# A two-layer hybrid attention trunk on one core: wider modulation products, a scaling moved to ScalarE, staggered value loads, and another scheduler for all instructions

## The chip, the core and the metric

The kernel runs on one core of one Trainium2 chip. The metric is the device time of an execution in microseconds (us). The core has TensorE (PE, matrix products; PEld are its weight loads), VectorE (DVE), ScalarE (ACT), GpSimd (POOL) and SyncE (SP), which here issues the DMAs. Each engine works through its own list of instructions strictly in order.

## What is computed

Two layers of a decoder trunk, sequence 512, width 1024, float32. Each layer, cut to what matters:

```python
shift, scale, gate = split(silu(c) @ w_ada + b_ada, 3)
h = rms_norm(x, ln_pre) * (1 + scale) + shift
u = split_columns(h @ w_in)          # 3740 columns: groups a, b, c, d
o_a = dilated_attention(a_q, a_k, a_v)
o_b = nsa_attention(b_q, b_kc, b_vc, b_ks, b_vs, b_kw, b_vw, b_g, ...)
o_c = rms_norm(gla_attention(c_q, c_k, c_v, log_sigmoid(c_a @ w_a2 + b_a) / 16), gla_norm)
o_d = banded_attention(d_q, d_k, d_v, window 128, sinks)
mixed = concat(o_a * silu(a_z), o_b * silu(b_z), o_c * silu(c_z), o_d * silu(d_z))
x = x + gate * rms_norm(mixed @ w_out, ln_post)
```

Group B compresses its keys and values by a small two-layer network (weights `w1`, `w2`) before it attends to them.

## The kernel before, in words

Every large product is made of three matmuls in a reduced-precision float form: the operand is split into a rounded part (`hi`) and a remainder (`lo`), and hi*hi, hi*lo and lo*hi are summed. So each piece of a weight (`wraw`, 128 x 1024 for most) is loaded, cast to `whi` on ScalarE (L475) and subtracted to `wlo` on VectorE (L478). The activations stand as `HH` and `HL`, transposed. `raw` holds four such loaded pieces, `w` three pairs of split ones.

**Start-up of layer 0** (`startup`, L659). x comes in four tiles of 128 rows. Each is squared and summed on ScalarE (L421), its reciprocal root is made on VectorE and GpSimd (L425, L426), and the tile is scaled on VectorE (L676). TensorE transposes it (L703), and the modulated result becomes `HH` and `HL` (L709 to L711). Shift and scale come from `mod` (L285): VectorE multiplies a weight tile `wmod` of 128 x 512 by the row silu(c) and sums it (L290), two halves for each of 16 columns. The weights of group C's first projections are used at once (`mms`, L719, L723).

**Projections** (`proj`, L641). 24 matmuls for each piece of 128 output columns (`mm_T`, L525), in the order of the list `CHUNKS`. While they run, the groups' attention is worked out.

**Group C** (`attn_c`, L811), gated linear attention without a sequential scan: six levels (64, 32, 16, 8, 4, 2 positions). At each level VectorE and ScalarE make decayed keys and queries `kq` (L922 to L926), TensorE makes scores `att` (L932), they are masked (L941), and TensorE multiplies them by values `vs` (L953). These values stand in another order than the projection leaves them: the projection's result goes to DRAM (`vd`, L571) and comes back as `vs`, two DMAs for each level (L824), all twelve issued at the start of the group. Ahead of the levels stands the log decay `la` (L836, L837) and its running sum `bp` (L841).

**Softmax units** (`unit`, L744): scores `sc` (L638, L639), mask and maximum on VectorE (L755), exponential on ScalarE (L757), scaling on VectorE (L766, L768), transposes `pT` on TensorE (L771), copies (L776, L778).

**Compression of group B** (`attn_b`, L1038): four `w1` loads fill the four raw buffers, TensorE makes `hid` (L1052), transposes it to `hT` (L1061), VectorE and ScalarE work out the gelu in some ten small steps on `hbuf`, TensorE makes `kcp` (L1080) and, from its split copy `kc`, the compressed scores `scmp` (L1097).

**Output** (`out1`, `out2`): the output projection `yo`, the second norm, the residual, the next layer's norm, transposes (L454) and its first projection (`mmTM`, L536). Norm of group C: `ms` (L972) from the split square `lo`.

**Background.** `extras` (L359) makes the next layer's modulation (32 products of `wmod`, L290) and this layer's gate (16 steps of `wada`, L348, L350) in small units with two buffers (`ad`).

**What sets the order.** The program is written in Python in a merged order: `merge` interleaves the groups with the projections by costs (the numbers after `yield` and the table `LP`). Then the tile scheduler reorders it: among instructions whose inputs are ready in its own model of the core, it takes the one with the best priority (program order, shifted by `tc.cur_priority`), engine by engine. The result is a fixed list for each engine and for SyncE's DMAs. `TLS = False` selects the scheduler's simple model of time; L1355 passes it on.

Of the kernel before, what the change touches and what calls it, by code (L numbers as in the profile page):

```python
# [19 lines left out]
PRE = 2  # L20
TLS = False
B = dict(raw=4, w=3, mx=3, v4=5, dv=2, ad=2, qk=16, g=8, p=3, sz=4, pt=3, sm=4)
QT = QH = QL = QG = 0
QX = 60
FIRST = 'xCwPxwxwxwTQc'
XH = 2
SG, MG = 1, 2
# [154 lines left out]
def pack(inp):  # L182
# [8 lines left out]
    for l in range(DEPTH):  # L191
# [10 lines left out]
        w_gate[l] = wa[:, 2048:].reshape(8, 128, 2, 512).transpose(2, 0, 1, 3)  # L202
        w_mod[l] = wa[:, :2048].reshape(2, 512, 2, 8, 128).transpose(3, 2, 0, 4, 1)
        for i, n in enumerate(('nsa_w1_k', 'nsa_w1_v')):
# [26 lines left out]
def build(tc, A, out_d):  # L231
    nc = tc.nc
    PE, ACT, DVE, POOL, SP = nc.tensor, nc.scalar, nc.vector, nc.gpsimd, nc.sync
    with ExitStack() as ctx:
# [44 lines left out]
        def load_mod(l, n, p, tag):  # L279
# [3 lines left out]
            return wt  # L283

        def mod(l, n, wt, ss, gs):  # L285

            o, c = _P['bada'][0], n // 2
            h = n % 2
            init, dst = (tmp[:, c:c + 1], ss[:, c:c + 1]) if h else (pars[l][:, o + c:o + c + 1], tmp[:, c:c + 1])
            DVE.tensor_tensor_reduce(wt, wt, csr[:, 512 * h:512 * h + 512], 0.5, init, ALU.mult, ALU.add, dst)  # L290
            if n % 4 == 3:
                j = n // 4
                o = _P['lnpre'][0]
                DVE.scalar_tensor_tensor(gs[:, j:j + 1], ss[:, c:c + 1], 1.0, pars[l][:, o + j:o + j + 1], op0=ALU.add, op1=ALU.mult)
# [9 lines left out]
        for ch in FIRST:  # L304
            if ch == 'C':
                SP.dma_start(out=cst[:, 0:256], in_=A['cst'][:, 0:256])
            elif ch == 'w':
                wmods.append(load_mod(0, len(wmods), qk_p, 'qk'))
            elif ch == 'P':
                load_par(0)  # L310
            elif ch == 'c':
                SP.dma_start(out=c_sb, in_=A['c'])
            elif ch in 'TQ':
                n = 'tm_c' if ch == 'T' else 't_cqk'
                WR[n] = [raw_p.tile([128, 1024 if ch == 'Q' else 996], F32, tag='raw', name='wraw')]
                SP.dma_start(out=WR[n][0], in_=A['w_in'][0, W_OFF[n, 0]:W_OFF[n, 0] + 128 * WR[n][0].shape[1]].rearrange('(p n) -> p n', p=128))
            else:
                i = len(x_t)
                t = v4_p.tile([128, 1024], F32, tag='v4', name=f'x{i}')
                for h in range(XH):  # L320
                    hs = slice(1024 // XH * h, 1024 // XH * (h + 1))
                    SP.dma_start(out=t[:, hs], in_=A['x'][128 * i:128 * i + 128, hs])
                x_t.append(t)
# [215 lines left out]

        def qk_t(name):  # L540
            return qk_p.tile([128, 512], F32, tag='qk', name=name)

# [32 lines left out]

        def qr_t(name):
            return qk_p.tile([128, 512], F32R, tag='qk', name=name)

        def fin_T(l, name, acc):
            par = pars[l]  # L580
            A0, B0 = slice(0, 64), slice(64, 128)
            if name == 'dka':

                kh, kl = qr_t('dkh'), qr_t('dkl')
                for hs in (A0, B0):
# [25 lines left out]
            elif name[0] == 'c':  # L611
                t = qk_t(name)
                ACT.activation(t, acc, AF.Copy, scale=32.0 ** -0.5 if name == 'cq' else 1.0)
                T[name] = t
            elif name[1] == 'q':

                x0, x1 = qr_t('x0'), qr_t('x1')
                ACT.copy(x0[A0], acc[A0])
# [4 lines left out]
            else:  # L623

                k0, k1, l0, l1 = qr_t('k0'), qr_t('k1'), qr_t('kl0'), qr_t('kl1')
                ACT.copy(k0[A0], acc[A0])
# [32 lines left out]
        def startup():  # L659

            tc.cur_priority -= SPX
            for i in range(4):
# [12 lines left out]
                else:  # L675
                    DVE.tensor_scalar(x_t[i], x_t[i], r, None, op0=ALU.mult)  # L676
            tc.cur_priority += SPX
# [12 lines left out]
            def macs(j):  # L690

                for n in range(4 * j, 4 * j + 4):
                    if len(wmods) <= n:
                        wmods.append(load_mod(0, n, qk_p, 'qk'))
                    mod(0, n, wmods[n], ss, gs)
                load_w(j)
# [114 lines left out]
        def attn_c(l):  # L811
# [7 lines left out]
            vss = {}  # L819
            for n, s in enumerate(LEVELS):  # L820
                vs = vsb[n // 3][:, 512 * (n % 3):512 * (n % 3) + 512].rearrange('p (i a n) -> p i a n', i=4, a=2)
                vss[s] = vs
                for e in range(2):
                    SP.dma_start(out=vs[64 * e:64 * e + 64].rearrange('p i a n -> p (i a n)'),  # L824
                                 in_=T['cvd'].rearrange('(m w r) e x -> w e m r x', w=2, r=s)[0, e])

            zp = ps_t('s', 'zp')
# [131 lines left out]
            for n, s in enumerate(LEVELS):  # L959
                nxt = level_scores(LEVELS[n + 1]) if n + 1 < len(LEVELS) else None  # L960
                level_values(s, at)
                at = nxt
# [75 lines left out]
        def attn_b(l):  # L1038
# [43 lines left out]
            PE.matmul(cp_[:, 64:128], hv, par[:, o:o + w], start=True, stop=True)  # L1082
            kct_ = qr_t('kc')
            kc = [kct_[:, 0:64], kct_[:, 64:128]]
# [62 lines left out]
        def wo_piece(l, n):  # L1147
# [4 lines left out]
            if k0 == 6:  # L1152
                res = []
                for j in range(kk):
                    r = raw[:, nc_ * j:nc_ * (j + 1)]
                    hi, lo = qr_t('wo2h'), qr_t('wo2l')
                    ACT.copy(hi, r)
# [208 lines left out]
```

## Time and profile before

| | |
|---|---|
| median of 3 runs | 694.81 us (694.17 to 696.92) |
| profiled execution | 697.9 us, of which the span from first to last instruction is 695.7 us |
| mean granted TensorE clock in the span | 0.986 of full |
| TensorE, VectorE, ScalarE busy | 93%, 72%, 48% of the span |
| HBM read, written | 81.88 MB, 5.24 MB |

How to read it: a busy share is an average over stages with different limits, and drawn matmuls overlap, so TensorE's busy time counts more than its work. The waits tell which engine stood still and for whom; the chain follows the last instruction back through whatever released each step. The granted clock is 1.00 at 2.4 GHz and 0.5 at 1.2 GHz, and a stretch's value is the mean of the two.

### The profile page before, as it was taken

Reading aid. Unit: us, or ns where it says so; the run is one execution under the profiler, and the core shown is the slowest. Engines: PE = TensorE matmul, PEld = TensorE weight load, DVE = VectorE, ACT = ScalarE, POOL = GpSimd, SP = SyncE. Lnnn points to the kernel's source line nnn. Section 1 sums busy time; section 2 is a strip of 40 time slices with the busy share of each in tenths; the row PEclk is TensorE's granted clock in tenths of the full one; section 3 lists DMA queues with packets and bytes.
Section 4 is the critical chain, followed back from the end, with each engine's and each line's share of the span. In section 5 each row is a group of like instructions: output and inputs, shape, how many; then the busy total and the mean of one; then the engine's idle time right before and its main releaser. Section 6 shows DMA issues by size and latency. Waiting matters only on the chain.

```text
span 695.7 us, 11980 instructions
## 1 busy us (share of the span) xinstructions
PE 649.8 (93%) x4460; PEld 524.5 (75%) x4460; DVE 498.6 (72%) x1291; ACT 336.8 (48%) x748; POOL 31.1 (4%) x57
## 2 busy tenths in 40 slices
PE   3999889989998999999998989899999999999996
PEld 1797766877777767779996768678777777778895
DVE  5985889666868787784598467743588878768656
ACT  5454444155565555663475244425545436435432
POOL 2000000000001100000012000000000000000000
PEclk9999999999999999999999999999999999999999
DMA  8955764657204444112642681212520021111143
GB/s 299 391 218 166 256 195 138 185 180 272 77 1 138 136 110 133 34 32 81 207 169 79 180 262 43 63 61 91 165 78 32 17 75 32 46 46 46 48 155 116
DMA packets 38163, 87.89 MB, mean 126 GB/s; under 512 B 4185, under 2 KB 7769, under 8 KB 38106
## 3 DMA queue, kind: packets, MB, share of 16 engines
q1 hardware_dynamic: 38106, 87.14, 38.7%
q8 instruction: 35, 0.57, 0.3%
q14 instruction: 22, 0.18, 0.1%
HBM read 81.88 MB, written 5.24 MB: 125 GB/s over the span
## 4 chain that ended last, share of the span: by engine, by line
PE 58%; DVE 17%; DMA 12%; ACT 6%; issue 4%; POOL 1%; SPq 1%; DVEq 0%; POOLq 0%; ACTq 0%
PE mmT L525 19%; PE yo L1169 9%; PE mmTM L536 5%; PE pT L771 5%; DMA wmod<-in_w_mod 4%; PE ob L785 3%; DMA vs<-vd 3%; DVE wlo L478 2%; DMA wraw<-in_w_in 2%; PE a L719 2%; PE yo L1216 2%; PE sc L638 2%; DVE wmod L290 2%; PE od L1007 2%; PE oa L785 2%
## 5 line engine op out<-in xcount | busy, mean ns | idle before, releaser
L525 PE MATMUL mmT<-HH,whi 128*128 128x512 f32 (+1 forms) x352 | 142.8, 406 | 1.4 <-ACT whi L475 1.4
L525 PE MATMUL mmT<-HH,wlo 128*128 128x512 f32 (+1 forms) x352 | 142.6, 405 | 0.4 <-DVE wlo L478 0.4
L525 PE MATMUL mmT<-HL,whi 128*128 128x512 f32 (+1 forms) x352 | 142.3, 404 | 0.0
L757 ACT ACTIVATE p<-p,m 128x256 f32<-128x256 f32 (+3 forms) x128 | 68.8, 538 | 66.9 <-DVE m L755 62.5
L478 DVE TENSOR_TENSOR wlo<-wraw,whi 128x1024 fp32r<-128x1024 f32 (+3 forms) x60 | 72.2, 1205 | 33.2 <-ACT whi L475 32.9
L475 ACT CAST whi<-wraw 128x1024 fp32r<-128x1024 f32 (+3 forms) x60 | 61.5, 1027 | 56.1 <-PE mmT L525 36.8
L525 PEld LDWEIGHTS mmT<-HH,wlo 128*128 128x128 f32 (+1 forms) x352 | 66.2, 188 | 16.1 <-issue 1.5
L525 PEld LDWEIGHTS mmT<-HH,whi 128*128 128x128 f32 (+1 forms) x352 | 66.4, 189 | 15.3 <-ACT whi L475 1.8
L525 PEld LDWEIGHTS mmT<-HL,whi 128*128 128x128 f32 (+1 forms) x352 | 66.4, 189 | 14.0 <-issue 1.2
L771 PE MATMUL pT<-cst,p 128*128 128x128 f32 x296 | 48.9, 279 | 6.0 <-DVE p L768 2.2
L536 PE MATMUL mmTM<-whi,HH 128*128 128x256 f32 (+1 forms) x160 | 48.6, 304 | 3.2 <-ACT HH L467 2.4
L755 DVE CUSTOM_DVE_ANT_0 p<-sc,cst 128x128 f32<-128x128 f32 (+3 forms) x96 | 44.8, 482 | 7.7 <-PE sc L639 7.3
L771 PEld LDWEIGHTS pT<-cst,p 128*128 128x128 f32 x296 | 33.3, 140 | 22.5 <-issue 11.8
L536 PE MATMUL mmTM<-whi,HL 128*128 128x256 f32 (+1 forms) x160 | 47.4, 297 | 0.4 <-DVE HL L468 0.4
L536 PE MATMUL mmTM<-wlo,HH 128*128 128x256 f32 (+1 forms) x160 | 47.2, 295 | 0.0
L1169 PE MATMUL yo<-wlo,HH 128*128 128x256 f32 x144 | 41.9, 291 | 0.0
L1169 PE MATMUL yo<-whi,HH 128*128 128x256 f32 x144 | 41.7, 290 | 0.0
L1169 PE MATMUL yo<-whi,HL 128*128 128x256 f32 x144 | 41.1, 286 | 0.0
L536 PEld LDWEIGHTS mmTM<-whi,HH 128*128 128x128 f32 x160 | 31.0, 194 | 6.1 <-ACT HH L467 3.5
L638 PE MATMUL sc<-k,x 128*128 128x128 f32 (+3 forms) x96 | 32.7, 352 | 0.5 <-DVE m L755 0.2
L778 DVE COPY pt<-pT 128x256 f32<-128x256 f32 (+3 forms) x60 | 28.4, 498 | 6.4 <-PE pT L771 5.5
L536 PEld LDWEIGHTS mmTM<-whi,HL 128*128 128x128 f32 x160 | 30.9, 194 | 1.9 <-DVE HL L468 0.9
(273 smaller groups left out, 1342.2 us busy)
## 6 DMA issues: line engine op xcount, KB each, us to landing
wraw<-in_w_in SPq DMA_DIRECT2D x52, 512.0 KB, 4.1
wmod<-in_w_mod SPq DMA_DIRECT2D x64, 256.0 KB, 5.4
wada<-in_w_gate SPq DMA_DIRECT2D x32, 256.0 KB, 3.1
wor<-in_w_out SPq DMA_DIRECT2D x12, 512.0 KB, 3.3
w<-in_w SPq DMA_DIRECT2D x8, 512.0 KB, 4.7
vs<-vd SPq DMA_DIRECT2D x24, 128.0 KB, 9.8
x<-in_x SPq DMA_DIRECT2D x8, 256.0 KB, 5.2
wor<-in_w_out SPq DMA_DIRECT2D x8, 256.0 KB, 2.9
```

Of the source, the lines that this page charges most:

```text
L290: DVE.tensor_tensor_reduce(wt, wt, csr[:, 512 * h:512 * h + 512], 0.5, init, ALU.mult, ALU.add, dst)
L475: ACT.copy(hi, raw)
L478: eng.tensor_tensor(out=lo, in0=raw, in1=hi, op=ALU.subtract)
L525: PE.matmul(acc[:m], a, b, start=(n == 0), stop=(n == 23))
L536: PE.matmul(acc[:, :ncol], a, b, start=(n == 0), stop=(n == 23))
L638: PE.matmul(out, q[e][:, qs], k[e][0][:, ks], start=True, stop=False)
L755: DVE.tensor_tensor_reduce(p[:, c], sc[:, c], mask, -0.125, 1e38 if sink is None else sink[0][:, es[j]:es[j] + 1], ALU.add, ALU.min, m[:, ...
L757: ACT.activation(p[:, c], p[:, c], AF.Exp, bias=m[:, j:j + 1], scale=-1.0, accum_out=lsum[:, j:j + 1])
L771: PE.transpose(tp[:, b:b + 128], p[:, b:b + 128], C('ident'))
L778: DVE.tensor_copy(dst, src)
L785: PE.matmul(o[hs, q0:q1], vt[:, kb, vc:vc + 64], PT[:, 512 * kb:512 * kb + q1 - q0], start=(first and kb == 0), stop=(last and kb == 3), s ...
L1169: PE.matmul(acc[:, :n_], a, b, start=(n == 0), stop=(n == last))
```

## The change

1. In layer 0 a modulation weight tile is 128 x 1024, one product for each column (`load_mod0`, `mod0`), not two halves; eight pair-wide buffers in `qk` take the place of sixteen. Other users of `qk` take their tiles as pairs (`qk_pair`), and the compressed key `kc` moves to the pool `g`.
2. In start-up the tiles of x are scaled on ScalarE. x is loaded whole, not in halves (`XH = 1`), and squared whole; the first loads stand in another order (`FIRST`).
3. In group C the loads of two levels are issued at the start, and those of level n+2 after the scores of level n+1.
4. `TLS = True`: the tile scheduler orders all instructions with its detailed timeline of the core.

```diff
-TLS = False
-B = dict(raw=4, w=3, mx=3, v4=5, dv=2, ad=2, qk=16, g=8, p=3, sz=4, pt=3, sm=4)
+TLS = True
+B = dict(raw=4, w=3, mx=3, v4=5, dv=2, ad=2, qk=8, g=8, p=3, sz=4, pt=3, sm=4)
...
-FIRST = 'xCwPxwxwxwTQc'
-XH = 2
+FIRST = 'xPwxCxwxwTQwc'
+XH = 1
...
+        def load_mod0(n):
+            wt = qk_p.tile([128, 1024], F32, tag='qk', name='wmod')
+            SP.dma_start(out=wt, in_=A['w_mod'][0, n // 2, n % 2].rearrange('a p n -> (a p n)').rearrange('(p n) -> p n', p=128))
+            return wt
+        def mod0(n, wt, ss, gs):
+            o, ln, j = _P['bada'][0], _P['lnpre'][0], n // 2
+            DVE.tensor_tensor_reduce(wt, wt, csr, 0.5, pars[0][:, o + n:o + n + 1], ALU.mult, ALU.add, ss[:, n:n + 1])
...
-        def qk_t(name):
-            return qk_p.tile([128, 512], F32, tag='qk', name=name)
+        def qk_pair(name, dt=F32R):
+            t = qk_p.tile([128, 1024], dt, tag='qk', name=name)
+            return t[:, 0:512], t[:, 512:1024]
...
-                    DVE.tensor_scalar(x_t[i], x_t[i], r, None, op0=ALU.mult)
+                    ACT.activation(x_t[i], x_t[i], AF.Copy, scale=r)
...
-                for n in range(4 * j, 4 * j + 4):
+                for n in range(2 * j, 2 * j + 2):
...
-            for n, s in enumerate(LEVELS):
+            def load_level(n):
+                s = LEVELS[n]
...
+            load_level(0)
+            load_level(1)
...
                 nxt = level_scores(LEVELS[n + 1]) if n + 1 < len(LEVELS) else None
+                if n + 2 < len(LEVELS):
+                    load_level(n + 2)
                 level_values(s, at)
...
-            kct_ = qr_t('kc')
+            kct_ = g_t('kc', [128, 128], F32R)
```

The lists of every engine change almost everywhere. Most line numbers are 16 to 22 higher after the change (L290 for the next layer is L306, L487 is L503, L922 is L942). Three places follow.

SyncE, layer 0, from the end of start-up to the first weight piece behind the value loads, before (`hb` is a constant, `par` the next layer's small parameters, `v_633` values for the smallest level):

```order
L487 DMA wraw<-in_w_in 128x1024
L740 DMA hb<-in_cst 128x128
L487 DMA wraw<-in_w_in 128x1024
L300 DMA par<-in_par 128x332
L571 DMA vd<-v_tm_c 128x4x128 x2
L282 DMA wmod<-in_w_mod 128x512 x2
L824 DMA vs<-vd 64x512
L817 DMA v_633<-vd 64x4x128 x2
L824 DMA vs<-vd 64x512
L824 DMA vs<-vd 64x1x512 x10
L282 DMA wmod<-in_w_mod 128x512
L487 DMA wraw<-in_w_in 128x1024
```

The same stretch now:

```order
L503 DMA wraw<-in_w_in 128x1024 x2
L756 DMA hb<-in_cst 128x128
L286 DMA wmod<-in_w_mod 128x512 x2
L588 DMA vd<-v_tm_c 128x4x128 x2
L286 DMA wmod<-in_w_mod 128x512
L842 DMA vs<-vd 64x512
L842 DMA vs<-vd 64x1x512
L833 DMA v_575<-vd 64x4x128 x2
L842 DMA vs<-vd 64x512
L842 DMA vs<-vd 64x1x512
L286 DMA wmod<-in_w_mod 128x512 x2
L503 DMA wraw<-in_w_in 128x1024
```

Two more full pieces stand ahead of this stretch than before (four ahead of `vd`, not two), and the next piece stands behind four value loads and not behind twelve.

VectorE, layer 0, one level of group C before:

```order
L922 TENSOR_TENSOR u<-b 128x256
L923 TENSOR_TENSOR u<-b 128x256
L478 TENSOR_TENSOR wlo<-wraw,whi 128x1024
L925 TENSOR_TENSOR kq<-ck,u 128x256
L290 ISA wmod,adass<-wmod,csr,tmp 128x512
L290 ISA adass 128x1
L926 TENSOR_TENSOR kq<-cq,u 128x256
L294 SCALAR_TENSOR_TENSOR adags<-adass,par 128x1
```

A level now:

```order
L961 TENSOR_TENSOR at<-att_862,cst 128x256
L942 TENSOR_TENSOR u<-b 128x256
L943 TENSOR_TENSOR u<-b 128x256
L961 TENSOR_TENSOR at<-att_863,cst 128x256
L646 TENSOR_TENSOR kl<-mmT,k_1078 64x512
L647 TENSOR_TENSOR kl<-mmT,k_1078 64x512
L306 ISA wmod,adass<-wmod,csr,tmp 128x512
L306 ISA adass 128x1
L945 TENSOR_TENSOR kq<-cqk,u 128x256
L946 TENSOR_TENSOR kq<-cqk,u 128x256
```

The modulation product no longer stands between the two halves of `kq`.

TensorE, layer 1, the compression of group B before (behind the last row 35 more rows of `mmT` stand ahead of `kcp`):

```order
L1052 MATMUL hid<-w_5132,x_4327 64x128
L1052 MATMUL hid<-w_5134,x_4453 64x128
L525 MATMUL mmT<-HL,whi 128x512
L525 MATMUL mmT<-HH,wlo 128x512
L1061 MATMUL hT<-cst,hbuf 128x128
L525 MATMUL mmT<-HH,whi 128x512
L525 MATMUL mmT<-HL,whi 128x512
L525 MATMUL mmT<-HH,wlo 128x512
```

And now:

```order
L1074 MATMUL hid<-w_5050,x_4367 64x128
L541 MATMUL mmT<-HH,wlo 128x512
L541 MATMUL mmT<-HH,whi 128x512
L541 MATMUL mmT<-HL,whi 128x512
L541 MATMUL mmT<-HH,wlo 128x512
L1083 MATMUL hT<-cst,hbuf 128x128
L1102 MATMUL kcp<-hbuf,par 64x32 x4
L1104 MATMUL kcp<-par,hbuf 128x64
L1119 MATMUL scmp_5133<-kc,x_4437 128x64
```

The projection matmuls between `hT`, `kcp` and `scmp` have gone to other places of the list.

## Rows read from the trace of the kernel before

**Rows 1.** The page, engine shares of the span and the chain by engine

```profile
PE 649.8 (93%) x4460; PEld 524.5 (75%) x4460; DVE 498.6 (72%) x1291; ACT 336.8 (48%) x748; POOL 31.1 (4%) x57
...
PE 58%; DVE 17%; DMA 12%; ACT 6%; issue 4%; POOL 1%; SPq 1%; DVEq 0%; POOLq 0%; ACTq 0%
```

**Rows 2.** Windows: stretch; each engine's busy us; PEclk, DMA share, GB/s

```profile
20.00:50.00 30.00, 29.35 (x156) 26.45 (x155) 29.00 (x78) 12.70 (x18) 1.96 (x5) 1.00 0.84 318
...
75.00:82.00 7.00, 6.35 (x26) 4.96 (x27) 5.98 (x12) 3.31 (x5) 0.00 (x0) 0.76 0.75 257
...
103.00:110.00 7.00, 7.00 (x103) 5.08 (x95) 5.86 (x15) 1.95 (x3) 1.22 (x2) 0.76 0.55 127
...
147.00:151.00 4.00, 4.00 (x13) 3.10 (x12) 2.55 (x6) 3.87 (x6) 0.27 (x2) 0.57 0.38 126
...
336.00:379.00 43.00, 38.85 (x265) 35.14 (x264) 35.40 (x76) 27.56 (x68) 6.72 (x12) 1.00 0.40 137
379.00:383.00 4.00, 4.00 (x19) 4.00 (x18) 2.92 (x3) 1.87 (x2) 1.02 (x3) 0.57 0.45 138
...
413.00:418.00 5.00, 4.34 (x19) 3.40 (x19) 3.22 (x7) 2.67 (x5) 0.00 (x0) 0.66 0.90 345
```

**Rows 3.** Groups of instructions: busy us, mean ns, idle before, releasers

```profile
L525 PE MATMUL mmT<-HH,whi 128*128 128x512 f32 x336 | 136.5, 406 | 1.4 <-ACT whi L475 1.4
...
L478 DVE TENSOR_TENSOR wlo<-wraw,whi 128x1024 fp32r<-128x1024 f32 x52 | 64.3, 1236 | 32.5 <-ACT whi L475 32.2
...
L475 ACT CAST whi<-wraw 128x1024 fp32r<-128x1024 f32 x52 | 54.6, 1049 | 54.9 <-PE mmT L525 36.8 <-DMA wraw<-in_w_in 11.4 <-PE mmTM L536 6.0
L771 PE MATMUL pT<-cst,p 128*128 128x128 f32 x296 | 48.9, 279 | 6.0 <-DVE p L768 2.2 <-ACT p L757 1.8 <-DVE l L763 1.1
...
L290 DVE CUSTOM_DVE_ANT_0 wmod<-wmod,csr,par 128x512 f32<-128x512 f32 x32 | 24.1, 760 | 9.3 <-DMA wmod<-in_w_mod 9.3
...
L932 PE MATMUL att<-kq 32*64 32x64 f32 x384 | 8.5, 225 | 5.4 <-DVE kq L926 3.3 <-DVE adags L294 2.0
...
L676 DVE TENSOR_SCALAR x<-x,rstd 128x1024 f32<-128x1024 f32 x4 | 3.0, 753 | 1.4 <-POOL rstd L426 1.3
```

**Rows 4.** Who waited for whom, PE: us in total, times, longest

```profile
PE tp L703 <- DVE x L676: 8.4, 4, 4.5
...
PE bp L841 <- DVE la L837: 3.0, 1, 3.0
PE mmTM L536 <- ACT HH L467: 2.4, 2, 1.8
...
PE ms L972 <- DVE lo L356: 2.1, 1, 2.1
...
PE mmT L525 <- ACT whi L475: 1.4, 1, 1.4
...
PE mmT L525 <- DVE wlo L478: 0.4, 1, 0.4
```

**Rows 5.** The chain that ended last: start us, us, what

```profile
58.48 10.86 DMA vs<-vd
69.36 4.77 DMA wraw<-in_w_in
...
599.45 2.97 PE mmT L525 x13
```

**Rows 6.** Timeline of VectorE, 88 to 108 us: start us, us, instruction

```profile
99.54 0.42 DVE L925 TENSOR_TENSOR kq<-ck,u 128x256 f32<-128x256 f32 x1
101.40 0.75 DVE L290 CUSTOM_DVE_ANT_0 wmod<-wmod,csr,tmp 128x512 f32<-128x512 f32 x1 [1.45 <-DMA wmod<-in_w_mod]
...
102.08 0.42 DVE L926 TENSOR_TENSOR kq<-cq,u 128x256 f32<-128x256 f32 x1
```

**Rows 7.** Timeline of TensorE, 490 to 508 us

```profile
495.13 0.27 PE L1061 MATMUL hT<-cst,hbuf 128*128 128x128 f32 x1
...
504.65 0.42 PE L1080 MATMUL kcp<-hbuf,par 128*64 128x32 f32 x8 [0.62 <-DVE hbuf L1072]
```

More of the change, by code (lines that the diff above doesn't have):

```diff
@@ L202, in pack @@
         w_gate[l] = wa[:, 2048:].reshape(8, 128, 2, 512).transpose(2, 0, 1, 3)
-        w_mod[l] = wa[:, :2048].reshape(2, 512, 2, 8, 128).transpose(3, 2, 0, 4, 1)
+        if l:
+            w_mod[l] = wa[:, :2048].reshape(2, 512, 2, 8, 128).transpose(3, 2, 0, 4, 1)
+        else:
+            w_mod[l] = wa[:, :2048].reshape(1024, 2, 8, 128).transpose(2, 1, 3, 0).reshape(8, 2, 2, 128, 512)
         for i, n in enumerate(('nsa_w1_k', 'nsa_w1_v')):
@@ L283, in load_mod @@
             return wt
+        def load_mod0(n):
[5 more added lines that the diff above has]
+            DVE.tensor_tensor_reduce(wt, wt, csr, 0.5, pars[0][:, o + n:o + n + 1], ALU.mult, ALU.add, ss[:, n:n + 1])
+            if n % 2:
+                DVE.scalar_tensor_tensor(gs[:, j:j + 1], ss[:, n:n + 1], 1.0, pars[0][:, ln + j:ln + j + 1], op0=ALU.add, op1=ALU.mult)
         def mod(l, n, wt, ss, gs):
@@ L307, in build @@
             elif ch == 'w':
-                wmods.append(load_mod(0, len(wmods), qk_p, 'qk'))
+                wmods.append(load_mod0(len(wmods)))
             elif ch == 'P':
@@ L574, in fin_tm @@
                     DVE.tensor_scalar(bg, bg, 0.5, 0.5, op0=ALU.mult, op1=ALU.add)
-        def qr_t(name):
-            return qk_p.tile([128, 512], F32R, tag='qk', name=name)
         def fin_T(l, name, acc):
@@ L582, in fin_T @@
             if name == 'dka':
-                kh, kl = qr_t('dkh'), qr_t('dkl')
+                kh, kl = qk_pair('dk')
                 for hs in (A0, B0):
@@ L611, in fin_T @@
             elif name[0] == 'c':
-                t = qk_t(name)
+                if name == 'cq':
+                    T['cqk_'] = qk_pair('cqk', F32)
+                t = T['cqk_'][name == 'ck']
                 ACT.activation(t, acc, AF.Copy, scale=32.0 ** -0.5 if name == 'cq' else 1.0)
@@ L615, in fin_T @@
             elif name[1] == 'q':
-                x0, x1 = qr_t('x0'), qr_t('x1')
+                x0, x1 = qk_pair('x01')
                 ACT.copy(x0[A0], acc[A0])
@@ L623, in fin_T @@
             else:
-                k0, k1, l0, l1 = qr_t('k0'), qr_t('k1'), qr_t('kl0'), qr_t('kl1')
+                (k0, k1), (l0, l1) = qk_pair('k01'), qk_pair('kl')
                 ACT.copy(k0[A0], acc[A0])
@@ L690, in macs @@
             def macs(j):
-                for n in range(4 * j, 4 * j + 4):
+                for n in range(2 * j, 2 * j + 2):
                     if len(wmods) <= n:
-                        wmods.append(load_mod(0, n, qk_p, 'qk'))
-                    mod(0, n, wmods[n], ss, gs)
+                        wmods.append(load_mod0(n))
+                    mod0(n, wmods[n], ss, gs)
                 load_w(j)
@@ L1155, in wo_piece @@
                     r = raw[:, nc_ * j:nc_ * (j + 1)]
-                    hi, lo = qr_t('wo2h'), qr_t('wo2l')
+                    hi, lo = qk_pair('wo2')
                     ACT.copy(hi, r)
```

## The prediction

> **What bounds the kernel now.** I read the page first, then the windows, the groups of instructions, the waits of TensorE, the chain, and two timelines. By the page TensorE is busy 93% of 695.7 us and VectorE 72% [rows 1]. That looks like a kernel with at most 45.9 us to win (695.7 - 649.8). But the chain that ended last gives TensorE only 58% of the span, VectorE 17%, DMA 12% and ScalarE 6% [rows 1]. The two differ because matmuls overlap: one projection matmul is drawn 406 ns long [rows 3], while thirteen in a row take 2.97 us, 228 ns each [rows 5]. So the busy share counts overlapped and stretched time, and the kernel is a long train of short waits among four in-order engines and one DMA queue. The Trainium skill says the same in "Perfetto Trace Analysis", section "Identifying the Most-Contended Engine": matmul busy time is a poor measure of headroom, the weight-load share is the better one. By that share, 75% here [rows 1], there is room for an order to win something; by the 93% there would be little. The rows side with the page of the skill, and the sum below needs only the rows.
>
> The clock is the second thing to see. TensorE's granted clock falls to the lower level (1.2 GHz) five times between 75 and 418 us: 0.76 over 7 us, 0.76 over 7, 0.57 over 4, 0.57 over 4 and 0.66 over 5 [rows 2]. Each time (1 - clock) x length is 1.7 us lost. Each follows a wait of TensorE of 1.4 to 3.0 us [rows 4], or of the 2 us at a level of group C. A removed wait of that size returns itself and 1.7 us.
>
> **The change part by part.**
>
> *Value loads two levels ahead.* In layer 0 the twelve value loads were issued in one block; the chain spends 10.86 us on them, and only then 4.77 us on the next weight piece [rows 5]. TensorE waited 1.4 us for its cast and 0.4 us for its remainder [rows 4]. In the new SyncE order four full pieces (group B's next four projections) stand ahead of vd, not two, and eight of the twelve value loads stand behind the first weight piece after it. Four pieces feed 96 matmuls, 96 x 0.228 = 21.9 us, and a 24-matmul piece goes before them: more than 10.86 + 4.77. So 1.8 goes, and 1.7 of clock: **-3.5 us**. In layer 1 two more pieces now stand ahead of the loads as well. There the late piece held up VectorE's remainder, and behind it the log-decay `la`, for which TensorE waited 3.0 us [rows 4], clock 1.7 [rows 2]: **-4.7 us**. The loads themselves are the same bytes; a level needs its own 3.5 scheduled units after it is asked for, and I cost that at nothing while the projections between the levels cover it. Without that cover each level would wait for about one load.
>
> *The order: levels of group C.* Before, VectorE's two key/query products of a level stood on either side of a next-layer modulation product: the first at 99.54, then 1.45 us idle for a DMA, the second at 102.08 [rows 6]. TensorE's `att` matmuls waited 5.4 us in all [rows 3] and a clock fall followed, 1.7 [rows 2]. Now all such pairs stand together, and between the score and value matmuls of a level some 20 projection matmuls stand at the first levels of either layer, where 4 to 13 did. I take all of it: **-7.1 us**. What is late next is the DMA of the product, which VectorE meets elsewhere with less behind it.
>
> *The order: softmax units.* TensorE waited 6.0 us for the probabilities it transposes [rows 3]. For each of the 88 units I added up the other TensorE work that stands between its last score matmul and its first transpose, at the steps of the trace (a 512-wide projection matmul 0.228, others in proportion): the median rises from 5.2 to 8.5 us, and units with less than 3 us fall from 12 to 1. I take the 6.0: **-6.0 us**. Bounds: 0 if VectorE is then the later one, and up to some 12 if the stretched records hide as much again.
>
> *The order: group C's norm.* 2.1 us for `lo` [rows 4] and 1.7 of clock; the new order has the same pattern there with more matmuls ahead of it. Half: **-1.9 us**.
>
> *Layer boundary.* 2.4 us for HH [rows 4] and 1.7 of clock [rows 2]. VectorE works 35.4 of 43 us there [rows 2]; the new order now puts each row's matmuls right behind its own transposes, with no cover of another row. Nothing taken, bounds -4 to +4.
>
> *1024-wide products.* 32 products of 0.760 us become 16. A 1024-wide two-input operation of VectorE takes 1.236 (the remainder) [rows 3], so 16 x (2 x 0.760 - 1.236) = 4.5 us of VectorE work goes, some three quarters of it between 20 and 50 us, where VectorE is busy 29.0 of 30 us [rows 2] and sets the pace: -3.4. But the new order puts three next-layer products among them, 3 x 0.76 = +2.3, and moves the large constant table and 0.5 MB of next-layer weights ahead of the last modulation weights in the queue. At 0.84 DMA share [rows 2] that queue has a little slack; cost nothing, up to +3 if it hasn't.
>
> *x scaled on ScalarE.* VectorE loses 4 x 0.753 [rows 3], but only while it waits for x anyway. The last tile is now loaded, squared and scaled whole. On ScalarE a 1024-wide cast takes 1.049 against 0.753 [rows 3], so the chain to the first transposes, for which TensorE waited 8.4 us in all [rows 4], grows by 0.3, and by about 1 more because the square no longer starts on a half. The Trainium skill speaks against this edit ("ScalarE: Activation LUTs", "Rules for kernel authors": multiply on VectorE, not ScalarE); its formula with one pointer operand gives 1.13 us, an estimate, so +0.4 in place of +0.3. The trace agrees on the direction. Until 50 us VectorE sets the pace, so I carry 0.6 of it. Start-up in sum: -3.4 + 2.3 + 0.6 = **-0.5 us**, bounds -4 to +4.
>
> *qk tiles as pairs.* Same bytes, same number of live pairs; nothing.
>
> *What it costs: the compression of layer 1.* Between `hT` at 495.13 (0.27 long) and `kcp` at 504.65 [rows 7] TensorE had 38 projection matmuls, 8.7 us at 0.228. The new order has none between `hT`, `kcp` and the compressed scores. The chain in between runs over VectorE, where three weight remainders still stand in front of it; these wait for casts and loads, since the four raw buffers have just held `w1`. 504.65 - 495.40 = 9.25; two gating products stand in that chain no more, 2 x 0.76 by the nearest row [rows 3]; 7.7, and 1.7 of clock: **+9.4 us**. Low end 4, if the remainders no longer wait; high end 12.
>
> Sum: -3.5 - 4.7 - 7.1 - 6.0 - 1.9 - 0.5 + 9.4 = -14.3. The profiled execution took 697.9 us (span 695.7), 3.1 above the median of 694.8. 697.9 - 14.3 = 683.6; on the footing of the median **680.5 us**, -2.1%. A measurement of this kernel tells about 0.5% (3.5 us) from no change: faster is below 691.3, slower above 698.3.
>
> **The rivals.**
>
> *Deeper.* VectorE also waits 9.3 us for the DMA of one half of its products [rows 3]; if the order takes this off the path, and the boundary's 4.1 and the other half of the norm with it, that is 15.3 more: 665 us. For it: the cover grows at nearly every unit. Against: VectorE's order still meets two-buffered loads, and it is not the engine that waits least.
>
> *Waits that change their name.* Half the gains come (11.9) against 9.4: 692 us. For it: VectorE is at 72% on average and above 80% in the levels and the boundary, so cover for TensorE may be a queue for VectorE. Against: the units of work on VectorE fall.
>
> *Starved projections, slower.* The new order spends prefetched weights early and stands without them later; it does so visibly at the compression of layer 1. A raw piece lands in some 4.8 us [rows 5], is cast in 1.05 and subtracted in 1.24 [rows 3], against 5.5 us of matmuls that it feeds, so with nothing ahead it can't be hidden. Each further hole of that kind costs 9.4. One more leaves 690; with two more the time is 680.5 + 18.8 = 699.3, slower. Places: the compression of layer 0, where the same four buffers hold `w1`, and the layer boundary. Against: waits for weights are 1.8 us before [rows 4], and in layer 0 24 matmuls still stand between `hT` and `kcp`.
>
> **How the numbers follow.** My forecast (670 to 691) has 0.48, deeper 0.16, changed names 0.16, slower 0.20. Faster: 0.48 + 0.16 + 0.02 of the third, 0.66; within 0.5%: 0.14; slower: 0.20. The range, 660 to 702, reaches into the deeper and the slower case (two holes) and leaves some 0.17 outside; my forecast's own range is 670 to 691.
>
> **What would show it.** Right: no wait for `whi` near 75 us and none for `la` near 410; `att` waits near nothing; idle before the transposes below 2 us; fewer than five clock falls; but a gap of 5 to 10 us at `kcp` in layer 1, with the clock low behind it; first projection matmuls a good 1 us later, start-up's end within 4 us. Wrong: mmT waiting for `whi` more than 10 us in all (starved), VectorE's wait for modulation weights grown, or a boundary longer by over 4 us. The sum is also wrong if TensorE's idle total falls by far more than 14 us, since then the stretched records hid waits that no row shows.

## The result, and the profile after

The changed kernel takes **756.34 us** (median of 4, 754.50 to 764.77) against 695.21 us: ratio **1.090**, 95% interval 1.081 to 1.099. It is slower by 61 us; forecast were 680.5 us and a range of 660 to 702.

The page of the changed kernel, engine shares and chain:

```profile
PE 659.8 (88%) x4460; PEld 540.0 (72%) x4460; DVE 492.1 (65%) x1255; ACT 337.0 (45%) x744; POOL 32.8 (4%) x57
...
PE 63%; DVE 14%; DMA 9%; issue 6%; ACT 5%; POOL 1%; SPq 0%; DVEq 0%; POOLq 0%; ACTq 0%
```

The same work stands in a longer span: TensorE's idle time goes from 45.9 [rows 1] to 92.9 us (752.7 - 659.8), while VectorE and ScalarE work no more than before. The second loss is the clock:

```profile
core 0: 752.7 us, clock 0.953
```

(1 - 0.953) x 752.7 = 35.4 us, where it was (1 - 0.986) x 695.7 = 9.7 before. The two losses overlap and can't be added: part of the low clock falls into idle time, where it costs nothing.

Where does it go? The windows cut both spans at the same places of the program: the first projection of layer 0, its first output projection, the first projection of layer 1 behind the boundary, layer 1's first output projection (columns as in [rows 2]). Before, then after:

```profile
0.00:52.20 52.20, 39.78 (x182) 31.88 (x183) 40.50 (x111) 25.85 (x48) 5.84 (x16) 1.00 0.83 303
52.20:301.00 248.80, 234.51 (x1622) 182.05 (x1621) 190.85 (x507) 127.70 (x289) 7.98 (x12) 0.98 0.46 142
301.00:383.70 82.70, 78.23 (x563) 70.85 (x563) 57.42 (x130) 44.75 (x110) 7.74 (x14) 0.98 0.36 118
383.70:630.90 247.20, 238.96 (x1652) 186.50 (x1652) 166.55 (x425) 113.61 (x235) 7.37 (x11) 0.99 0.26 84
630.90:695.70 64.80, 58.30 (x447) 53.19 (x446) 43.25 (x121) 24.84 (x70) 2.19 (x4) 0.98 0.29 98
```

```profile
0.00:56.60 56.60, 39.20 (x182) 30.73 (x183) 38.67 (x85) 28.48 (x42) 6.03 (x16) 1.00 0.85 324
56.60:324.20 267.60, 236.73 (x1566) 185.18 (x1565) 176.35 (x446) 119.65 (x257) 9.81 (x12) 0.94 0.40 123
324.20:430.80 106.60, 87.45 (x619) 79.92 (x618) 70.93 (x188) 51.06 (x144) 7.71 (x12) 0.90 0.34 108
430.80:691.90 261.10, 242.76 (x1668) 193.96 (x1668) 168.22 (x438) 117.17 (x248) 7.06 (x13) 0.97 0.24 75
691.90:752.70 60.80, 53.63 (x431) 50.24 (x429) 37.92 (x102) 20.59 (x57) 2.19 (x4) 0.98 0.27 92
```

Start-up +4.4, layer 0 +18.8, the boundary +23.9, layer 1 +13.9, the end -4.0: 57.0, the whole difference of the spans. The cuts are at the same instructions, not after the same work: by the counts of matmuls, 56 that stood ahead of layer 0's first output projection now stand behind it (1622 to 1566, 563 to 619), and 16 have moved from the end into layer 1. So some us of the boundary's +23.9 belong to layer 0, and of layer 1's +13.9 to the end. The waits of TensorE in the changed kernel:

```profile
PE mmTM L552 <- ACT HH L483: 15.4, 4, 7.7
PE mmT L541 <- DVE x L637: 10.9, 5, 3.0
PE kcp L1102 <- DVE hbuf L1094: 8.1, 1, 8.1
PE tp L719 <- ACT x L692: 7.4, 3, 3.3
PE zp L850 <- issue: 7.3, 1, 7.3
PE sc L654 <- DVE m L771: 4.1, 8, 1.0
PE att L952 <- DVE kq L946: 3.7, 5, 1.8
```

The waits for `la` and `lo` of [rows 4] are gone, that for `HH` is six times as long, and new ones stand beside it. Three places show how.

*Layer 0, ahead of the log decay.* VectorE's timeline; `dk` and `ca` come from one projection, and `zp` needs `ca`:

```profile
63.91 0.68 DVE L601 TENSOR_TENSOR dk<-mmT,dk 64x512 fp32r<-64x512 f32 x1
71.68 0.75 DVE L306 CUSTOM_DVE_ANT_0 wmod<-wmod,csr,tmp 128x512 f32<-128x512 f32 x1 [7.10 <-DMA wmod<-in_w_mod]
...
73.14 0.69 DVE L601 TENSOR_TENSOR dk<-mmT,dk 64x512 fp32r<-64x512 f32 x1
73.86 0.69 DVE L605 COPY ca<-mmT 16x512 f32<-16x512 f32 x1
```

A modulation product of the next layer, in no hurry, waits 7.10 us for its weights; behind it stand the second half of `dk` and `ca`, and TensorE waits 7.3 us at `zp`. From 66 to 84 us the granted clock is 0.72 (first row; the others are for the places below):

```profile
66.00:84.00 18.00, 10.66 (x37) 8.46 (x36) 9.41 (x20) 5.64 (x9) 0.00 (x0) 0.72 0.79 240
...
386.00:431.00 45.00, 25.99 (x126) 23.60 (x125) 28.40 (x60) 19.75 (x50) 4.29 (x8) 0.77 0.37 120
554.50:560.00 5.50, 4.70 (x26) 4.41 (x27) 3.01 (x10) 1.20 (x3) 0.00 (x0) 0.50 0.30 95
```

*The boundary* (second row above): TensorE is busy 25.99 of 45 us at a clock of 0.77. The chain there, around one row of 128 tokens:

```profile
391.29 4.79 DMA wada<-in_w_gate
...
396.95 3.38 DMA wada<-in_w_gate
...
405.61 5.63 PE mmTM L552 x24
...
411.27 0.38 ACT v_tm_c L577
...
411.67 0.23 DVE dv L579
411.90 0.32 DVE hf L480
...
412.61 0.65 DVE yg L1254 x2
...
415.69 0.70 DVE HL L484
...
416.43 4.89 PE mmTM L552 x22
```

The projection of one row, its result read out, and only then VectorE's work on the transposes of the next row, its remainder `HL`, its projection: almost nothing overlaps. The first matmuls of the last three rows stand at 405.61, 415.54 and 424.68 us, 9.9 and 9.1 us apart. Ahead of 405.61 the chain is another: VectorE meets gate products (`aac`, L366) that wait for their loads `wada`, and behind them stands the next row's work; there TensorE's wait for `HH` is longest, 7.7 us. Before, output projections of later rows stood between the transposes of earlier ones, until 359.9 us:

```profile
347.88 1.09 PE L454 MATMUL tp<-cst,y 128*128 128x128 f32 x8 [0.73 <-DVE y L438]
348.73 0.47 PE L1169 MATMUL yo<-wo2l,HH 128*128 128x512 f32 x1
...
356.13 1.09 PE L454 MATMUL tp<-cst,y 128*128 128x128 f32 x8 [0.31 <-DVE y L438]
```

*Compression of layer 1*, as foreseen:

```profile
546.14 0.27 PE L1083 MATMUL hT<-cst,hbuf 128*128 128x128 f32 x1
554.50 0.64 PE L1102 MATMUL kcp<-hbuf,par 128*64 128x32 f32 x8 [8.10 <-DVE hbuf L1094]
```

### The profile page after: what moved, and what is told of

Same layout as the page of the kernel before. It is cut to its first block, busy times and chain, and to the rows that moved or that the text cites. A ratio compares the mean times of both kernels' runs of the same rounds, so it can differ in the third digit from the quotient of the medians.

```text
span 752.7 us, 11904 instructions
## 1 busy us (share of the span) xinstructions
PE 659.8 (88%) x4460; PEld 540.0 (72%) x4460; DVE 492.1 (65%) x1255; ACT 337.0 (45%) x744; POOL 32.8 (4%) x57
## 4 chain that ended last, share of the span: by engine, by line
PE 63%; DVE 14%; DMA 9%; issue 6%; ACT 5%; POOL 1%; SPq 0%; DVEq 0%; POOLq 0%; ACTq 0%
PE mmT L541 27%; PE yo L1191 9%; PE mmTM L552 6%; DMA wada<-in_w_gate 4%; PE pT L787 4%; PE ob L801 3%; DMA wmod<-in_w_mod 2%; DVE wlo L494 2%; PE yo L1238 2%; PE sc L654 2%; PE a L735 2%; PE sc L655 2%; ACT whi L491 2%; PE oa L801 1%; DVE aac L366 1%
## 5 line engine op out<-in xcount | busy, mean ns | idle before, releaser
L541 PE MATMUL mmT<-HH,whi 128*128 128x512 f32 (+1 forms) x352 | 145.2, 413 | 14.0 <-DVE x L637 10.9
L541 PEld LDWEIGHTS mmT<-HH,whi 128*128 128x128 f32 (+1 forms) x352 | 68.2, 194 | 33.3 <-issue 7.6
L541 PEld LDWEIGHTS mmT<-HH,wlo 128*128 128x128 f32 (+1 forms) x352 | 67.9, 193 | 17.0 <-DVE wlo L494 1.3
L541 PEld LDWEIGHTS mmT<-HL,whi 128*128 128x128 f32 (+1 forms) x352 | 68.2, 194 | 14.3 <-issue 0.2
L552 PE MATMUL mmTM<-whi,HH 128*128 128x256 f32 (+1 forms) x160 | 51.7, 323 | 16.5 <-ACT HH L483 15.4
L552 PE MATMUL mmTM<-whi,HL 128*128 128x256 f32 (+1 forms) x160 | 50.7, 317 | 3.6 <-DVE HL L484 3.6
L794 DVE COPY pt<-pT 128x256 f32<-128x256 f32 (+3 forms) x60 | 29.4, 500 | 35.0 <-PE pT L787 30.2
L552 PE MATMUL mmTM<-wlo,HH 128*128 128x256 f32 (+1 forms) x160 | 50.0, 312 | 0.0
L787 PE MATMUL pT<-cst,p 128*128 128x128 f32 x296 | 46.7, 277 | 2.1 <-DVE p L784 1.5
L552 PEld LDWEIGHTS mmTM<-whi,HH 128*128 128x128 f32 x160 | 33.6, 210 | 18.7 <-ACT HH L483 16.3
L552 PEld LDWEIGHTS mmTM<-whi,HL 128*128 128x128 f32 x160 | 33.7, 211 | 5.9 <-DVE HL L484 4.9
```

Source lines behind the costliest of these rows:

```text
L541: PE.matmul(acc[:m], a, b, start=(n == 0), stop=(n == 23))
L552: PE.matmul(acc[:, :ncol], a, b, start=(n == 0), stop=(n == 23))
L787: PE.transpose(tp[:, b:b + 128], p[:, b:b + 128], C('ident'))
L794: DVE.tensor_copy(dst, src)
```

## The experiments

Each ratio is to the kernel before, measured beside it (medians of 694.9 to 696.9 us). Differences between two runs are of their medians; where the kernel before moved between them, they are good to 1 or 2 us.

**The parts alone.** Theory A: the order lost the time. B: another part did. C: only their meeting does.

*Order alone.* `TLS = True` in the kernel before.

> The kernel before with one word changed: the scheduler's detailed timeline orders it. Theory A (the order lost the 61 us, since it stands chains of VectorE and DMA without cover at the layer boundary, at the compression of layer 1 and in layer 0): 745 to 770 us, with waits for HH and hf at the boundary of over 15 us in all. Theory B (the order wins what I forecast and one of the other three parts lost more): 680 to 692 us, without the waits at the boundary. Theory C (the order loses only together with the later value loads or the paired buffers): 700 to 735 us.

742.80 us, ratio 1.067 (1.064 to 1.070): +45.9 us, theory A, a little under its range. The boundary takes 108.0 us, and its waits are there:

```profile
PE mmTM L536 <- ACT HH L467: 12.5, 4, 4.8
...
PE mmTM L536 <- DVE HL L468: 4.1, 4, 2.8
```

*The other parts with the old scheduler.* `TLS = False` in the changed kernel.

> The changed kernel with the simple scheduler: 1024-wide products, x on ScalarE, value loads two levels ahead. Theory A: 683 to 695 us, the loads worth some 4 to 8 us and the start-up within 4. Theory B: 735 us or more. Theory C: 685 to 700 us.

703.51 us, 1.011 (1.008 to 1.013): +6.6. None of the gain that A left to these parts, and far from B's 735; A's own range for it is missed too.

*Value loads alone*, in the kernel before:

```diff
-            for n, s in enumerate(LEVELS):
+            def load_level(n):
+                s = LEVELS[n]
...
+            load_level(0)
+            load_level(1)
...
+                if n + 2 < len(LEVELS):
+                    load_level(n + 2)
```

> The kernel before with the value loads two levels ahead alone, simple scheduler. My prediction: -3.5 us in layer 0 (no wait for whi near 75 us) and -4.7 in layer 1 (no wait for la near 410 us), so 685 to 689 us. Rival (a level then waits for its own load, or the pieces are no earlier): 693 us or more, with a wait for vs on the chain.

703.73 us, 1.009 (1.007 to 1.011): **+6.8 where -8.2 was forecast**. The rival's number, but not its reason. VectorE's timeline of this kernel:

```profile
61.21 0.69 DVE L591 COPY ca<-mmT 16x512 f32<-16x512 f32 x1
67.52 0.75 DVE L290 CUSTOM_DVE_ANT_0 wmod<-wmod,csr,par 128x512 f32<-128x512 f32 x1 [5.62 <-DMA wmod<-in_w_mod]
...
68.31 0.69 DVE L839 TENSOR_SCALAR la<-zp 128x512 f32<-128x512 f32 x1
```

Before, the second pair of next-layer weights was issued behind the block of value loads (at 67.77 us), and its products stood behind `la` (at 78.3). Now it is issued behind the first value loads (at 57.84), lands no earlier than 67.5 us, and its product stands ahead of `la`. In layer 1 a gate product waits 5.11 us in front of `ca` in the same way.

*Products and x.* The changed kernel with the old scheduler and all value loads at the start.

> The changed kernel with the simple scheduler and all twelve value loads at the start of the group: what is left is the 1024-wide products, paired buffers and x on ScalarE. My prediction: -3.4 + 0.6 = -2.8 us, so 690 to 694 us. Rival (the modulation weights bound start-up, not VectorE): within 1 us of before. Rival (the first matmuls come later by more than VectorE wins): 696 us or more.

696.86 us, 1.000 (0.997 to 1.002): nothing. The first projection ends at 50.8 us, 1.4 earlier than before, and nothing of that is left in the median.

*Products alone*: the kernel of the run before, with `XH = 2`, the old `FIRST`, x on VectorE.

> The kernel before with 1024-wide products and paired buffers alone: x on VectorE in halves and the first loads in the old order, simple scheduler. If the products win 3.4 us and x on ScalarE gives them back: 691 to 694 us. If neither does anything here: 695 to 698 us. If the paired buffers or the larger loads cost: 699 us or more.

695.61 us, 0.999 (0.996 to 1.001): nothing either. So x on ScalarE took nothing back that the products had won.

Order 45.9, value loads 6.8, products and x 0.0 make 52.7. The whole is 61.1; the rest is theirs together (layer 0 takes 258.2 us with the order alone, 267.6 with all; start-up 53.6 and 56.6). The parts aren't independent: with the order alone, too, a next-layer product waits 7.93 us for its weights in front of the second half of `la`.

**The product ahead of the log decay.** Theory H: that product is the price of the later loads. The hold makes it depend on `la`, so that it can't stand ahead:

```diff
             DVE.tensor_tensor(out=la, in0=la, in1=t1, op=ALU.subtract)
+            DVE.tensor_scalar(T['hold'], la[:, 0:16], 0.0, None, op0=ALU.mult)
...
+            DVE.tensor_tensor(out=cs, in0=csil, in1=hold[:, 0:8], op=ALU.add)
+                DVE.tensor_tensor(out=pb, in0=pars[l + 1][:, ob_:ob_ + 16], in1=hold, op=ALU.add)
```

Gate products read `cs`, modulation products start from `pb`. The edit does one thing more: `extras` begins only when the hold exists, so the background's loads move back in program order as well. No run separates the two.

> The kernel before; the background products (next layer's modulation, gate) take a factor or addend made from the log decay la, times zero, so that none can stand ahead of la on VectorE; nothing is left out. Theory H (a background product that waits for its own load in front of la is what the later value loads cost): the kernel before has such waits only in layer 1 (1.3 to 2.6 us each), so a gain of 2 to 5 us, 692 to 695. Rival (the products only wait elsewhere, with as much behind them): within 1 us or slower.

692.95 us, 0.995 (0.993 to 0.998). The size is H's, the place isn't. H saw such waits in layer 1 alone, but by the windows it is layer 0 that gets shorter (248.8 to 241.2 us; in front of `la` VectorE waited at most 0.8 us for a product there), and layer 1 gets longer (247.2 to 250.3). In layer 0 TensorE's waits for `whi` (1.4) and `adags` (2.0) are gone. So this gain is not shown to be H's, and that it fell into H's range is luck.

> Value loads two levels ahead alone, as in the run of that name, with the same hold. Theory H: the two waits of 5.6 and 5.1 us and the clock behind them go, so at least 8 us less than without the hold: 688 to 695 us, and not slower than the kernel before with the hold. Rival (the later value loads cost by themselves, at the levels or by the order of the queue): still 5 us or more above the kernel before with the hold.

692.97 us, 0.995 (0.993 to 0.997): 10.8 us less than without the hold, and the same as the run before it. For the later loads H holds: the waits of 5.62 and 5.11 us are gone, and with the hold the later loads by themselves are worth nothing.

> Products, x on ScalarE and value loads with the simple scheduler, with the same hold. Theory H: 8 us or more below the same without the hold (which was 1.05% above the kernel before): 687 to 696 us. Rival: no change from it, 700 to 705 us.

696.92 us, 1.000 (0.998 to 1.002): 6.6 less than without, a little short of what H expected.

> The kernel before ordered by the detailed timeline (742.8 us), with the hold at la. If the wait of 7.9 us for a next-layer weight in front of la in layer 0 costs what it did in the changed kernel: 733 to 737 us. If the products then stand in front of something as late: 740 us or more.

736.27 us, 1.059: 6.5 less than the order alone.

> The changed kernel with the same hold. Theory H for its share of the loss: the wait of 7.1 us for a next-layer weight ahead of la in layer 0 goes with its clock (some 10 us), and the gate products of layer 1 leave the boundary (4.7 us of waits and six products of 0.75): 735 to 748 us. Rival (the order loses by standing each row's transposes behind the matmuls of the row before, and by stretches without cover, whatever the background does): 748 to 757 us, boundary as long as in the changed kernel.

748.61 us, 1.075 (1.070 to 1.080): 7.7 less, just over H's range. Here the windows tell another story than the log decay: the boundary gets 7.9 us shorter (106.6 to 98.7), since the gate products have left it, layer 0 only 4.4 (267.6 to 263.2), and layer 1 5.2 longer (261.1 to 266.3). In layer 0 TensorE no longer waits at `zp`, but the next-layer product waits again, one step behind `la`:

```profile
83.29 0.75 DVE L306 CUSTOM_DVE_ANT_0 wmod<-wmod,csr,pb 128x512 f32<-128x512 f32 x1 [6.31 <-DMA wmod<-in_w_mod]
...
86.18 0.42 DVE L888 TENSOR_TENSOR u<-u 128x256 f32<-128x256 f32 x1
```

TensorE's `dp` waits 5.5 us for this `u`. With the new order a hold at `la` mostly moves the wait, as the rival to H had it for the kernel before; the order alone with the hold shows the same (layer 0 7.8 us shorter, the boundary 7.5, layer 1 8.7 longer). In sum the hold returns 6.5 to 10.8 us in these four; 52 stay in the changed kernel.

*Hold in layer 0 alone*, in the kernel before (`if l == 0` around both places).

> The kernel before with the hold in layer 0 alone, simple scheduler. By stages the hold in both layers won 7.6 us in layer 0 and lost 3.1 in layer 1, where the gate's products then met the levels. So without it in layer 1: 688 to 692 us, faster than either kernel and than the hold in both. Rival (the layers aren't independent, layer 1's gain of the hold at la of 3 us goes too): 693 to 696 us.

**690.76 us, 0.993 (0.991 to 0.995)**: faster than either kernel by a little, as expected. VectorE there:

```profile
66.93 0.69 DVE L847 TENSOR_TENSOR la<-la,t 128x512 f32<-128x512 f32 x1 [1.39 <-ACT t L845]
...
68.47 0.75 DVE L290 CUSTOM_DVE_ANT_0 wmod<-wmod,csr,pb 128x512 f32<-128x512 f32 x1
...
76.63 0.74 DVE L290 CUSTOM_DVE_ANT_0 wmod<-wmod,csr,tmp 128x512 f32<-128x512 f32 x1
```

The first product comes right behind `la`, the second 8 us later, after most of the head of group C.

**Where the order loses.** The further runs start from the changed kernel with the hold (748.61), all behind the first with its ties as well; one control starts from the kernel before.

*Ties at the boundary.* Transposes whose results are overwritten, five by the code and by the count of matmuls (4465 against 4460):

```diff
+                if nxt is not None and c == 0 and i > 1:
+                    PE.transpose(acc[:, 0:128], ys[i - 2][:, 896:1024], C('ident'))
...
+                if i < 3:
+                    PE.transpose(acc[:, 0:128], YS[l - 1][i + 1][:, 896:1024], C('ident'))
```

> The changed kernel with the hold, and with seven small transposes that tie TensorE's list at the layer boundary: the second part of the output projection of row i waits for the normed row i-2, and the next layer's first projection of row i for the normed row i+1 (their results are overwritten). Theory A1 (the new order spends the output projection at once and then stands each row's chain naked): from the first yo to the first projection of layer 1 some 12 us less than with the hold alone (98.7), 83 to 88, and 732 to 740 us in all. Rival (VectorE's chain over four rows bounds the boundary, whatever TensorE's order): 96 us or more there and 746 us or more in all.

741.61 us, 1.064 (1.061 to 1.067): 7.0 less, 92.5 us at the boundary. Between the two: of the 16 us by which the boundary was still longer than before (98.7 against 82.7), 6 were the order of TensorE. For the rest TensorE now waits at the transposes, 8.4 us for the normed rows.

> The kernel before with the hold (692.95 us) and the same ties at the boundary. Its order has the cover there already, so theory A1 expects nothing: 691 to 695 us, first yo to first projection 80 to 83 us. If the small transposes or the tie itself cost, as a rival for any loss seen in the run with the ties on the changed kernel: 696 us or more.

698.34 us, 1.004 (1.002 to 1.006): the ties cost some 5 us where there is nothing to win, so what they returned above may be understated.

*Later hold*, with the ties: made from the last level's scores `at`.

```diff
+                if nxt is None:
+                    DVE.tensor_scalar(T['hold'], at[:, 0:16], 0.0, None, op0=ALU.mult)
```

> The changed kernel with the ties at the boundary (741.6 us), but the hold made from the last level's masked scores in place of la: no background product of a layer can stand before the end of group C's levels. Theory B (the new order runs the background as soon as its loads are in, in the middle of the levels' chain: eight gate products there in layer 1): the levels, from the first att to the last, fall from 42.7 and 40.1 us to about 33 in each layer, and 725 to 735 us in all. Rival (the products only move on, into the softmax units, with as much behind them): levels shorter, but 738 to 748 us.

730.18 us, 1.051 (1.048 to 1.055): 11.4 less, theory B. The levels, which took 42.70 and 40.10 us, now:

```profile
92.40:122.60 30.20, 29.86 (x464) 25.00 (x458) 17.80 (x36) 12.16 (x21) 2.68 (x4) 1.00 0.17 54
453.80:483.60 29.80, 29.29 (x470) 24.99 (x462) 17.21 (x35) 13.09 (x22) 2.44 (x4) 1.00 0.18 55
```

The rival has its part: layer 0 falls from 265.0 to 244.4 us, below the 248.8 of the kernel before, but the boundary grows from 92.5 to 106.2, where 28 more matmuls and the last gate products of layer 0 (to 310.2 us) now stand.

*Pace.* With the ties: all projections tied to softmax units (or levels) by a one-column matmul on the row maximum (or the scores) three units back.

```diff
+            if len(MARK) >= 3:
+                PE.matmul(acc[:, 0:1], C('ident'), MARK[-3], start=True, stop=True)
```

> The run before it, and each projection of group a to d also waits for the row maximum (or level) of the softmax unit three back in program order, by a one-column matmul whose result is overwritten: so the projections can't be spent ahead of the units that need them as cover. Theory A2 (the new order spends cover early: 455 and 460 projection matmuls left behind the last level of layer 0 and 1, where the kernel before has 519 and 538): a further 8 to 25 us, 708 to 728 us. Rival (the loss inside the layers lies in VectorE's order, not in the cover): within 4 us of the run before it, 728 to 744 us.

776.39 us, 1.115 (1.112 to 1.118): 35 us **more**, outside both ranges. Theory A2, that projections are spent too early as cover, gets no support; but the tie also holds projections back at the levels, and there TensorE waits 9.4 us for `kq` and 8.0 for `at`, so the run doesn't test A2 alone.

*The end of layer 1*: such a tie, to the unit just ahead, for its last two projections alone.

> The changed kernel with hold and boundary ties (741.6 us); in layer 1 the last two projections (48 matmuls, 11 us) also wait for the row maximum of the softmax unit just ahead of them in program order. In the run with the ties alone the last projection ends 12.8 us before the output projection of layer 1 begins, with units alone in between. Theory A2 in its small form (that stretch is naked for want of cover): 4 to 9 us less, 732 to 738 us. Rival (a tie to VectorE makes TensorE wait for it, as when all projections were tied): 741 us or more.

747.46 us, 1.074 (1.066 to 1.082): 5.9 more. The last projection now ends 1.5 us before the output projection, but layer 1 is no shorter (268.1 against 266.6 us). In this form A2 falls.

*Group C's norm off VectorE*:

```diff
-                DVE.tensor_tensor(out=on, in0=oc[hp], in1=rs, op=ALU.mult)
+                ACT.copy(on, oc[hp])
+                POOL.tensor_tensor(out=on, in0=on, in1=rs, op=ALU.mult)
```

> The changed kernel with hold and boundary ties (741.6 us); group C's last product on, for which VectorE stands idle 31.4 us in four places, is copied by ScalarE and multiplied on GpSimd, so that VectorE's list no longer stands behind it. Theory V (VectorE's list holds instructions too early, and what stands behind them is late for TensorE): 5 to 15 us less, 727 to 737 us, with TensorE's waits for x and sz after the levels (13.4 us in all) at half. Rival (VectorE then waits as long at the next head of its list, since the chain behind on is late anyway): 738 to 746 us.

741.75 us, 1.066 (1.063 to 1.070): no change, the rival. The waits of VectorE, ahead of which `on` stood with 31.4 us:

```profile
DVE sz L574 <- ACT th L572: 24.4, 3, 8.3
DVE pt L802 <- PE pT L795: 20.7, 12, 5.4
```

The next instruction of the list, a gate `sz`, waits in its place.

**What stays open.** Of 61 us, hold, ties and later hold return 26 (to 730.18). Of the other 34 one piece is known, the hole at the compression of layer 1, where TensorE still waits 7.9 us at `kcp`. By the windows layer 0 is now shorter than before; the boundary is 23.5 us longer (106.2 against 82.7, with 83 more matmuls in it) and layer 1 14.9 (262.1 against 247.2). Why, is not settled: the three other attempts, made without the later hold, won nothing.

## Why the prediction was wrong

To set the terms beside the result, I took all 4460 matmuls in the order of their ends and summed, by name and stage, by how much each step exceeds the usual one of its kind (the 30th percentile over both traces). This is TensorE's lost time with its clock in it: 111.0 us before, 167.2 after, a difference of 56.2 of the 57.0. The two totals shift with what is counted as one kind; the difference doesn't.

| late matmul, stage | before | after | change | forecast |
|---|---|---|---|---|
| `pT`, softmax units | 13.2 | 6.7 | -6.5 | -6.0 |
| `ms`, norm of group C | 2.7 | 0.4 | -2.3 | -1.9 |
| `bp`, log decay, layer 1 | 4.1 | 0.0 | -4.1 | -4.7 |
| `kcp`, `scmp`, compression, layer 1 | 0.9 | 11.8 | +10.9 | +9.4 |
| `att`, levels | 10.8 | 9.7 | -1.1 | -7.1 |
| `zp` and projections ahead of the levels, layer 0 | 4.8 | 12.9 | +8.1 | -3.5 |
| `tp`, `a`, start-up | 16.9 | 21.3 | +4.4 | -0.5 |
| `mmTM`, boundary | 5.4 | 27.1 | +21.7 | 0 |
| projections behind the levels | 7.9 | 22.7 | +14.8 | none |
| `sc`, scores of the units | 3.2 | 8.6 | +5.4 | none |
| `oc`, `mmTM`, in the levels | 5.6 | 13.7 | +8.1 | none |

- **Right, by name and size:** softmax units, norm, log decay of layer 1, and the hole at the compression of layer 1. Two of these gains were lost again close by: the units' scores `sc` lost 5.4 more, and the projections ahead of the levels of layer 1 4.9 where it was 0.6.
- **Value loads, the step that failed first.** The wait for `whi` went as said, but "the loads themselves are the same bytes", costed at nothing, was wrong: what moved with them was a background load, and its product on VectorE. The rows printed ahead of the prediction show next-layer weights among the value loads; whose product stands behind them on VectorE I didn't ask. The price was +6.8 alone, where -8.2 was forecast.
- **Layer boundary, the largest miss.** "Nothing taken, bounds -4 to +4": I had read that each row's matmuls stand behind its own transposes with no cover, and costed it at zero with bounds that came from the old waits (2.4 and 1.7), not from the length of the chain laid bare. The chain takes 9.9 and 9.1 us a row, for 24 matmuls that need 3.6 at full clock (24 x 0.15, their step before). The gate products that wait for their loads between two rows were in no term; without them (the hold) the boundary is 7.9 us shorter. A boundary longer by over 4 us was one of the prediction's own signs of being wrong.
- **The order: levels.** -7.1 taken in full; the pairs of key/query products do stand together, but in layer 0 the background went into the same chain elsewhere (47.1 us for the levels, 104.2 to 151.3; 30.2 in the run with the later hold).
- **What the sum left out.** Projections behind the levels and scores lost 20.2 us, which no term had. The sum priced the waits of the old trace that would vanish, and looked for new ones at a single place. A new order of all engines makes new waits everywhere; the old trace can't show those, and the count of cover (5.2 to 8.5 us) only spoke of one kind.
- **Start-up** +4.4 lies just outside its bounds (-4 to +4). A 1024-wide product took 1.280 us, not 1.236. Scaling x on ScalarE took 1.144 by the row below. The Trainium skill's formula ("ScalarE: Activation LUTs", "What ACT_TABLE_LOAD costs") gave 1.13, an estimate, and the trace agrees. With the old order these edits made start-up 1.4 shorter, and the order alone made it 1.4 longer; the +4.4 comes only with both.

```profile
L692 ACT ACTIVATE x<-x,rstd 128x1024 f32<-128x1024 f32 x4 | 4.6, 1144 | 2.9 <-POOL rstd L431 2.9
...
L297 DVE CUSTOM_DVE_ANT_0 wmod<-wmod,csr,par 128x1024 f32<-128x1024 f32 x16 | 20.3, 1280 | 0.7 <-DMA wmod<-in_w_mod 0.7
```

- **The rivals.** "Slower" had the sign, but not the mechanism: TensorE waits 0.6 us for `whi` and 0.9 for `wlo` in all, nothing is starved. What happened is "waits that change their name", but that rival stopped at a gain of 2.8 us and the kernel lost 61: I bounded it by the gains, as if new waits could at worst eat what was won.

Why the order is what it is, the lists of the built programs tell in part. Under the simple scheduler, changing one of three priority shifts (`QT` to `QG`, `QX`, `SPX`) moves rows of the lists; under the timeline each moves none, while the groups' priority `HC` still does. So these shifts, set for the boundary and the start-up, no longer act. Whether that is what lost the time, and whether the timeline's times for loads are off, no run here shows.

## What to carry to other kernels

When a change reorders everything, read the new lists for who stands in front of whom at each step that many wait for (here the log decay and the layer boundary), and ask of each instruction in front what it may wait for; the old trace prices only the waits that vanish. Background work that waits for its own load can be tied behind such a step by a data dependence: a multiply by zero and two small additions in layer 0 won 0.7% here. Then look where the wait went: tied one step too early, the product waits in front of the next step, and in layer 1 the same tie lost time. Change the scheduler in a run of its own: of four parts one made three quarters of the loss.

## What the runs showed of the hardware that was not expected

A load of 256 KB that was issued behind six value loads landed late: in the run with the later value loads SyncE issued it at 57.84 us and its product began at 67.52, 9.7 us later, where the median of these loads from issue to landing is 5.7. Issuing it earlier only moved its waiting product ahead of what mattered. And a short hole costs more than itself: the granted clock fell during the 8.1 us at `kcp`, and in the 5.5 us behind the hole (554.5 to 560.0) it was still 0.50, at most another 2.8 us.
